# Gates and merge of the mix layers: from feature-major groups of 256 columns to token-major groups of 512

## The chip, the cores and the metric

The kernel runs on one core of one Trainium2 chip. The metric is the device time of one execution in microseconds (us). The core has five engines with queues of their own: PE (matrix products; its weight loads are shown apart as PEld), DVE (vector), ACT (activation functions and copies), POOL and SP (here the issuer of the weight loads). Matrix products are written to PSUM, of which the kernel uses eight banks of 128 partitions x 512 f32 values in the mix layers.

## The reference

The model is a stack of six layers on 256 tokens of width 1024: mix, feed-forward, mix, mixture of experts, and two more. The change touches the two mix layers only. Cut to what matters:

```python
h = _rmsnorm(x, norm_mix[l])
p_rw, p_sb, p_ret, p_conv = jnp.split(h @ w_in[l], MIX_SPLITS, axis=-1)
branches = (rwkv7(p_rw), stick_breaking(p_sb), retention(p_ret), conformer_conv(p_conv))   # each 256 x 256
merged = sigmoid(h @ w_gate[l, 0]) * (branches[0] @ w_branch[l, 0])
for i in range(1, 4):
    merged = merged + sigmoid(h @ w_gate[l, i]) * (branches[i] @ w_branch[l, i])
x = x + merged @ w_out[l]
```

Each gate is a product 256 x 1024 by 1024 x 1024, each branch product 256 x 256 by 256 x 1024. The sigmoid is computed as (1 + tanh(z/2)) / 2, and the last factor of one half is applied once, when the merged features are split.

## The kernel before

All large products are done in three passes of reduced-width f32 (`mm3`, L302): every operand z is split (`split`, L291) into a high part by ACT and the rest, a low part, by DVE, and high x high, high x low and low x high are added in PSUM. The weights come as raw blocks of 128 x 1024 f32 (512 KB) by DMA from SP's queue (L166) into four buffers, and are split into three pairs of buffers (`whi`, `wlo`); `_WS.next` hands out the next 128, 256 or 512 columns of a block. The normed input is kept feature-major, as tiles `hh` and `hl` of 128 features x 8 chunks x 256 tokens.

There are two forms of product. `gemm_f` is feature-major: a block of 128 x 128 weights is stationary and the 256 tokens stream, so its result has features on partitions; a group has two feature chunks, 2 x 8 x 3 matmuls, in one PSUM bank. `gemm_t` is token-major: 128 tokens of `hh`/`hl` are stationary and 512 weight columns stream; its result has tokens on partitions, and it fills two banks, one for each half of the tokens, step by step in turn. Both take their banks from the pool `mmt` of three banks. The other five banks are those of the mixers: three in the lane `mr` (RWKV) and two in the lane `mx`.

In `mix_layer` the generator `jobs` issues the input products and then the gates 3, 2, 1 (L640 is their tanh, into the tiles `gth`). Beside it the four mixers run as threads, which are let in between two steps of a product. L627 and L631 are the evacuations of the three products ahead of the gates (rq twice, and the retention gate `gs`, whose tanh at L631 needs the buffer `w0`, which the convolution's norm uses too). Then `merge` issues, in the order of the list `MERGED`, gate 0 (its tanh is L660) and the branch products in quarters of 256 features: first the four quarters of gate 0, then for each quarter the branches 2, 1, 3 and, one quarter later, 0. DVE multiplies each branch product by its gate (L664) and adds it to the sum (L666); after branch 0 of a quarter, the sum is split (L293, L294) into `m`, which is feature-major and so is right away the stationary operand of the output projection `out_proj` (matmuls `op`): it streams 512 columns of `w_out` for two halves q of the columns, eight chunks k and two halves t of the tokens.

The order in an engine's queue is not the program's order alone: when the kernel is built, instructions of each engine are put in order by priority (early in the program first) and by when a simulated timeline has their inputs and buffers ready.

Of the kernel before, what the change touches and what calls it, by code (L numbers as in the profile page):

```python
# [11 lines left out]
F32 = mybir.dt.float32  # L12
F32R = mybir.dt.float32r
BF16 = mybir.dt.bfloat16
I32 = mybir.dt.int32
AF = mybir.ActivationFunctionType
ALU = mybir.AluOpType
# [3 lines left out]
T = 256  # L21
D = 1024
KT = 8
# [13 lines left out]
W1 = 7  # L37
MERGE = 2, 1, 3, 0

MERGED = [(None, _c) for _c in range(4)]  # L40
for _c in range(4):
    MERGED += [(_i, _c) for _i in MERGE[:-1]] + [(MERGE[-1], _c - 1)] * (_c > 0)
MERGED += [(MERGE[-1], 3)]
RW_SCALE = 0.606531
NEWTON = -0.703952253
SS_SCALE = 1.0 / (16.0 * -NEWTON ** 3)
# [163 lines left out]
class _K:  # L210
# [166 lines left out]
        return ps  # L377


    def gemm_t(self, ws, h, part=lambda t: slice(t * 128, (t + 1) * 128)):  # L380
        hh, hl = h
        if ws.w == 512:
            ps = [self.mmt("gt").rearrange("p a b -> p (a b)") for t in range(2)]
            for k in range(KT):
                w = ws.next()
                for t in range(2):
                    self.mm3(ps[t], hh[:, k, part(t)], hl[:, k, part(t)], *w, k == 0, k == KT - 1)
                    yield
            return ps
        ps = self.mmt("gt")  # L390
        blocks = [ws.next() for k in range(KT)]
        for t in range(2):
            s = part(t)
            for k in range(KT):
                self.mm3(ps[:, t, :], hh[:, k, s], hl[:, k, s], *blocks[k], k == 0, k == KT - 1)
                yield
        return ps
# [85 lines left out]
        self.scaled = xi  # L483
        return last

    def out_proj(self, ap, h, nk=KT, norm=True, out=None, skew=2, spare=()):

        nc = self.nc
        hh, hl = h
        skew += len(spare)  # L490
        ws = _WS(self, ap, 512, {nk - skew + i: z for i, z in enumerate(spare)})
        ps = {}

        def products(t, q, k, w):
            s = slice(t * 128, t * 128 + 128)
            if (t, q) not in ps:
                ps[t, q] = self.mmt("op").rearrange("p a b -> p (a b)")
            return self.mm3(ps[t, q], hh[k][:, s], hl[k][:, s], *w, k == 0, k == nk - 1)

        def finish(t, q):  # L500
            c = slice(q * 512, q * 512 + 512)
            self.held["add"] = nc.vector.tensor_add(self.x[:, t, c], self.x[:, t, c], ps[t, q])
            if out is not None:
                nc.sync.dma_start(out.rearrange("(t p) d -> p t d", t=2)[:, t, c], self.x[:, t, c])
            elif norm:
                self.summed = (self.sumsq(t, q, ps[t, q]),)

        late = []
        for q in range(2):
            for k in range(nk):  # L510
                w = ws.next()
                products(0, q, k, w)
                yield
                if q * nk + k >= 2 * (nk - skew):
                    late.append((q, k, w))
                else:
                    products(1, q, k, w)
                    yield
            finish(0, q)
            if q == 0 and not late:  # L520
                finish(1, q)
        for q, k, w in late:
            self.held["mm", (q - 2) * nk + k + 2] = products(1, q, k, w)
            yield
            if k == nk - 1:
                finish(1, q)
        if not late:
            finish(1, 1)


    def mix_layer(self, l):
        nc, tc = self.nc, self.tc
        with ExitStack() as ctx:
            p = lambda name, **k: _Pool(ctx.enter_context(tc.tile_pool(name=self.nm(name), reuse_waits="tile", **k)))

            bp, gp, lp = p("bp", bufs=1), p("gp", bufs=3), p("lp", bufs=1)
# [33 lines left out]
            wi, wg = self.a[f"w_in_{l}"], self.a[f"w_gate_{l}"]  # L570
            xn = gp.tile([128, 2, D], F32, tag="gth", name=self.nm("xn"))
            h = self.norm_tiles()
            brt = lambda tag: lp.tile([128, 2, 2, T], F32R, tag=tag, name=self.nm("br"))
            br, gth = [None] * 4, [None] * 4

            def jobs():
# [12 lines left out]
                for i in range(4):  # L589
                    ps = yield from self.gemm_f(wf, h)  # L590
                    for j in range(2):
                        f = 2 * i + j
# [39 lines left out]
                nc.vector.scalar_tensor_tensor(gs, th, 1.0, ps, op0=ALU.add, op1=ALU.mult)  # L632
                ret.append((rq, gs))
                for i in (3, 2, 1):
                    gth[i] = gp.tile([128, 2, D], F32, tag="gth", name=self.nm("gth")).rearrange(
                        "p a (b c) -> p (a b) c", c=T)
                    ws = _WS(self, wg[8 * i - 8:8 * i], 128)
                    for fp in range(4):
                        ps = yield from self.gemm_f(ws, h)
                        nc.scalar.activation(gth[i][:, 2 * fp:2 * fp + 2, :], ps, AF.Tanh, scale=0.5)  # L640

            ret = []

# [4 lines left out]

            def merge():

                ws = _WS(self, self.a[f"w_merge_{l}"], 128)
                q4 = self.tp.tile([128, 2, 2, T], F32, tag="q4", name=self.nm("g0"))
                g0 = [self.tp.tile([128, 2, T], F32, tag=n, name=self.nm("g0")) for n in ("hs", "hc")] + [q4[:, 0], q4[:, 1]]
                mg, mh, ml = gth[MERGE[0]], [], []
                for i, fp in MERGED:
                    s = slice(2 * fp, 2 * fp + 2)
                    o = mg[:, s, :]
                    if i is None:
                        ps = yield from self.gemm_f(ws, h)
                        nc.scalar.activation(g0[fp], ps, AF.Tanh, scale=0.5)  # L660
                        continue
                    gt = gth[i][:, s, :] if i else g0[fp]
                    ps = yield from self.gemm_f(ws, (br[i][:, 0], br[i][:, 1]), 2)
                    nc.vector.scalar_tensor_tensor(gt, gt, 1.0, ps, op0=ALU.add, op1=ALU.mult)  # L664
                    if i != MERGE[0]:
                        nc.vector.tensor_add(o, o, gt)  # L666
                    if i == MERGE[-1]:
                        m = self.rp.tile([128, 2, 2, T], F32R, tag=("MB", "Tn", "Tt", "AR")[fp], name=self.nm("m"))
                        self.split(o, m[:, 0], m[:, 1], scale=0.5)
                        for j in range(2):  # L670
                            mh.append(m[:, 0, j, :])
                            ml.append(m[:, 1, j, :])
                pair = lambda *t: lambda: [lp.tile([128, D], F32R, tag=n, name=self.nm("wx")) for n in t]
                yield from self.out_proj(self.a[f"w_out_{l}"], (mh, ml), spare=(pair("C", "E"), pair("A", "B")))

            self.run(jobs())
            self.run(merge())
# [1206 lines left out]
def _blocks(w, n, order="f"):  # L1884

    k, c = w.shape
    b = w.reshape(k // 128, 128, c // n, n)
    b = b.transpose(1, 2, 0, 3) if order == "f" else b.transpose(1, 0, 2, 3)
    return np.ascontiguousarray(b.reshape(128, -1, min(1024, b[0].size)).transpose(1, 0, 2))


def _pack(i):
# [6 lines left out]
    for l in range(L):  # L1899
        w = i["w_in"][l]  # L1900
        col = lambda a, b: w[:, a * 256:b * 256]
        f[f"w_in_{l}"] = np.concatenate(
            [_blocks(col(0, 4), 128), _blocks(col(11, 13), 128), _blocks(col(7, 9), 128), _blocks(col(10, 11), 128),
             _blocks(np.concatenate([col(9, 10), col(6, 7)], 1), 512), _blocks(col(4, 6), 512)], 0)
        f[f"w_gate_{l}"] = np.concatenate([_blocks(i["w_gate"][l, b], 128) for b in range(1, 4)], 0)
        wb, g0 = i["w_branch"][l], i["w_gate"][l, 0]
        f[f"w_merge_{l}"] = np.concatenate(
            [_blocks((g0 if b is None else wb[b])[:, 256 * c:256 * c + 256], 128).transpose(1, 0, 2).reshape(128, -1)
             for b, c in MERGED], 1).reshape(128, -1, 1024).transpose(1, 0, 2).copy()
        f[f"w_out_{l}"] = _blocks(i["w_out"][l], 512)  # L1910
        lo = np.zeros((128, 768), np.float32)
        lo[0:64, 0:256] = i["rw_w2"][l]
        lo[64, 0:256] = i["rw_w0"][l]
        lo[64:128, 256:512] = i["rw_a2"][l]
        lo[:, 512:768] = i["rw_g2"][l]
        f[f"lora_{l}"] = lo
        two = lambda v: np.concatenate([v, v])[:, None]
        f[f"par1_{l}"] = np.concatenate(
            [_fm(i["rw_mu"][l]), _fm(i["rw_a0"][l]), _fm(i["rw_k_k"][l]),
             _fm(i["rw_k_a"][l]), _fm(i["rw_r_k"][l].reshape(-1)), _fm(i["rw_ln_w"][l]), _fm(i["rw_ln_b"][l]),  # L1920
             two(i["sb_q_norm"][l]), two(i["sb_k_norm"][l]), _fm(i["ret_gn"][l]), _fm(i["conv_b"][l]),
             _fm(i["conv_ln_w"][l]), _fm(i["conv_ln_b"][l]),
             i["conv_dw"][l].T.reshape(2, 128, 31).transpose(1, 0, 2).reshape(128, 62)], 1)
# [64 lines left out]
```

## Time and profile before

| | us |
|---|---|
| median of 3 runs (1624.14 to 1625.99) | 1625.78 |
| the profiled execution | 1624.98 |
| its span, first to last instruction | 1622.8 |
| PE busy | 1590.9 |
| DVE busy | 1236.9 |
| ACT busy | 949.4 |

An engine's busy time counts instructions in flight. Matmuls are pipelined, so a busy PE is not PE at its peak: the time between the starts of two matmuls says more than the duration of one. In rows of a timeline the columns are the start in us, the duration in us, the engine, the line, the operation, the output and its inputs by the program's names, the shapes, the count, and in brackets the idle time before it with what ended that.

### The profile page before, as it was taken

How to read it: one execution, taken by the hardware profiler on the slowest of the kernel's cores; microseconds unless marked ns; L12 is line 12 of the kernel's file. 1: busy time of each engine (PE TensorE's matmuls, PEld its weight loads, DVE VectorE, ACT ScalarE, POOL GpSimd, SP SyncE). 2: the span in 40 equal slices, each digit the busy share in tenths (PEclk: the TensorE clock that was granted, in tenths of full speed). 3: DMA queues.
4: the chain of work that ended last, by engine and by line, in shares of the span. 5: the costliest groups of instructions: out<-in, count | busy, mean ns of one | idle time of the engine just before them, and what ended most of it. 6: DMA issues, size and time to landing. Idle time of an engine off the chain costs nothing.

```text
span 1622.8 us, 28866 instructions
## 1 busy us (share of the span) xinstructions
PE 1590.9 (98%) x11229; PEld 1394.3 (86%) x11229; DVE 1236.9 (76%) x2017; ACT 949.4 (59%) x1414; POOL 98.2 (6%) x183
## 2 busy tenths in 40 slices
PE   7999999999999999998999999999999999999998
PEld 6999998999889999997788788888789987888887
DVE  5698678655565996687989989899877776796775
ACT  4545444544446464345877878878756565554654
POOL 2000000100000000001000000100110000010020
PEclk9999999999999999999999999999999999999999
DMA  7443345555555433354989989999754343444342
GB/s 272 154 179 108 118 140 185 200 183 182 195 169 183 169 126 110 120 177 171 349 314 337 362 307 345 353 330 362 266 169 156 116 145 119 141 167 137 129 143 91
DMA packets 89452, 323.71 MB, mean 199 GB/s; under 512 B 10208, under 2 KB 10384, under 8 KB 89312
## 3 DMA queue, kind: packets, MB, share of 16 engines
q1 hardware_dynamic: 86832, 313.89, 55.3%
q0 software_dynamic: 1616, 5.47, 1.0%
q10 hardware_dynamic: 864, 2.47, 0.4%
q8 instruction: 89, 1.46, 0.4%
q14 instruction: 51, 0.42, 0.1%
HBM read 320.74 MB, written 1.05 MB: 198 GB/s over the span
## 4 chain that ended last, share of the span: by engine, by line
PE 49%; DVE 2%; issue 1%; ACT 1%; DVEq 0%; ACTq 0%
PE eg L302 13%; PE gt L302 10%; PE ye L302 7%; PE gf L302 7%; PE op L302 3%; PE s L302 2%; DVE wlo L291 1%; PE seg L302 1%; PE sc L302 1%; PE ms L302 1%; PE xg L302 1%; PE mo L302 1%; PE ut L313 1%; PE qkT L313 1%; ACT whi L291 0%
## 5 line engine op out<-in xcount | busy, mean ns | idle before, releaser
L291 DVE TENSOR_TENSOR wlo<-raw,whi 128x1024 fp32r<-128x1024 f32 x579 | 704.7, 1228 | 256.1 <-ACT whi L291 246.0
L291 ACT ACTIVATE whi<-raw 128x1024 fp32r<-128x1024 f32 x579 | 608.2, 1059 | 413.2 <-PE gf L302 148.2
L302 PE MATMUL gf<-hh,whi 128*128 128x256 f32 x1408 | 400.9, 285 | 0.1
L302 PE MATMUL gf<-hh,wlo 128*128 128x256 f32 x1408 | 400.9, 286 | 0.0
L302 PE MATMUL gf<-hl,whi 128*128 128x256 f32 x1408 | 400.7, 285 | 0.0
L302 PEld LDWEIGHTS gf<-hl,whi 128*128 128x128 f32 x1408 | 269.5, 191 | 2.9 <-issue 1.5
L302 PEld LDWEIGHTS gf<-hh,wlo 128*128 128x128 f32 x1408 | 268.6, 191 | 3.6 <-issue 1.8
L302 PEld LDWEIGHTS gf<-hh,whi 128*128 128x128 f32 x1408 | 269.5, 191 | 1.9 <-issue 0.4
L302 PE MATMUL eg<-wlo,Xh 128*128 128x512 f32 (+1 forms) x384 | 145.8, 380 | 3.2 <-DVE wlo L291 3.2
L302 PE MATMUL eg<-whi,Xl 128*128 128x512 f32 (+1 forms) x384 | 144.1, 376 | 0.0
L302 PE MATMUL eg<-whi,Xh 128*128 128x512 f32 (+1 forms) x384 | 140.1, 382 | 1.4 <-DVEq L1289 1.4
L302 PE MATMUL gt<-whi,hh 128*128 128x512 f32 (+1 forms) x368 | 128.3, 354 | 2.6 <-ACT whi L291 1.5
L302 PE MATMUL gt<-wlo,hh 128*128 128x512 f32 (+1 forms) x368 | 129.7, 353 | 1.1 <-DVE wlo L291 1.1
L302 PE MATMUL gt<-whi,hl 128*128 128x512 f32 (+1 forms) x368 | 128.5, 350 | 1.4 <-DVE hl L291 1.4
L302 PEld LDWEIGHTS eg<-wlo,Xh 128*128 128x128 f32 x384 | 72.1, 188 | 19.8 <-DVE wlo L291 7.3
L302 PEld LDWEIGHTS eg<-whi,Xh 128*128 128x128 f32 x384 | 72.1, 188 | 15.3 <-ACTq L1289 1.6
L302 PEld LDWEIGHTS eg<-whi,Xl 128*128 128x128 f32 x384 | 72.4, 189 | 12.6
L302 PEld LDWEIGHTS gt<-whi,hh 128*128 128x128 f32 x368 | 70.3, 192 | 12.9 <-ACT hh L291 2.2
L302 PEld LDWEIGHTS gt<-whi,hl 128*128 128x128 f32 x368 | 70.3, 191 | 12.4 <-DVE hl L291 2.7
L302 PEld LDWEIGHTS gt<-wlo,hh 128*128 128x128 f32 x368 | 70.5, 192 | 11.2 <-DVE wlo L291 1.9
L302 PE MATMUL ye<-wlo,uh 128*128 128x512 f32 x176 | 69.2, 393 | 0.0
L302 PE MATMUL ye<-whi,ul 128*128 128x512 f32 x176 | 69.0, 392 | 0.0
(516 smaller groups left out, 2431.9 us busy)
## 6 DMA issues: line engine op xcount, KB each, us to landing
raw<-in_moe_w SPq DMA_DIRECT2D x264, 512.0 KB, 5.2
raw<-in_ffn_w SPq DMA_DIRECT2D x66, 512.0 KB, 3.3
raw<-in_even_w_in SPq DMA_DIRECT2D x65, 512.0 KB, 3.3
raw<-in_w_in SPq DMA_DIRECT2D x52, 512.0 KB, 4.2
raw<-in_w_gate SPq DMA_DIRECT2D x48, 512.0 KB, 3.2
raw<-in_w_merge SPq DMA_DIRECT2D x32, 512.0 KB, 3.2
raw<-in_odd_w_in SPq DMA_DIRECT2D x32, 512.0 KB, 3.3
raw<-in_w_out SPq DMA_DIRECT2D x16, 512.0 KB, 3.2
```

Source lines behind the costliest of these rows:

```text
L291: return nc.scalar.activation(hi, src, AF.Copy), nc.vector.tensor_sub(lo, src, hi.bitcast(F32))
L302: return self.nc.tensor.matmul(out, lhsT, rhs, **kw)
L313: return self.nc.tensor.transpose(out, z, self.c("ident") if ident is None else ident)
```

## The change

The gates 3, 2, 1, gate 0 and the branch products become token-major with 512 columns: `gemm_t` with the normed input (or a branch) stationary, in halves c of 512 features. `gemm_t` gets a number of chunks `nk` and a `lane`: for the branch products (nk=2) the bank of the second token half comes from the lane `mx`. `MERGED` gets a new order: half 0 of gate 0, branches 2, 1, 3 of half 0, half 1 of gate 0, branch 0 of half 0, then branches 2, 1, 3, 0 of half 1. The merged sum now has tokens on partitions, so `turn(c)` transposes it on PE, 128 x 128 at a time, into a bank of the lane `mr`, and splits it from there: `turn(0)` stands ahead of the third last group of the list, `turn(1)` in the output projection ahead of chunk 4. The host packs the same weights in the new order.

```diff
-MERGED = [(None, _c) for _c in range(4)]
-for _c in range(4):
-    MERGED += [(_i, _c) for _i in MERGE[:-1]] + [(MERGE[-1], _c - 1)] * (_c > 0)
-MERGED += [(MERGE[-1], 3)]
+MERGED = [(None, 0)] + [(_i, 0) for _i in MERGE[:-1]] + [(None, 1), (MERGE[-1], 0)] + [(_i, 1) for _i in MERGE]
+TURN = 3
...
-    def gemm_t(self, ws, h, part=lambda t: slice(t * 128, (t + 1) * 128)):
+    def gemm_t(self, ws, h, part=lambda t: slice(t * 128, (t + 1) * 128), nk=KT, lane=None):
         hh, hl = h
         if ws.w == 512:
-            ps = [self.mmt("gt").rearrange("p a b -> p (a b)") for t in range(2)]
-            for k in range(KT):
+            ps = [self.mx("gt", lane) if t and lane else self.mmt("gt").rearrange("p a b -> p (a b)") for t in range(2)]
+            for k in range(nk):
                 w = ws.next()
                 for t in range(2):
-                    self.mm3(ps[t], hh[:, k, part(t)], hl[:, k, part(t)], *w, k == 0, k == KT - 1)
+                    self.mm3(ps[t], hh[:, k, part(t)], hl[:, k, part(t)], *w, k == 0, k == nk - 1)
...
-    def out_proj(self, ap, h, nk=KT, norm=True, out=None, skew=2, spare=()):
+    def out_proj(self, ap, h, nk=KT, norm=True, out=None, skew=2, spare=(), before=None):
...
             for k in range(nk):
+                if before and q == 0 and k == before[0]:
+                    before[1]()
                 w = ws.next()
...
-                    gth[i] = gp.tile([128, 2, D], F32, tag="gth", name=self.nm("gth")).rearrange(
-                        "p a (b c) -> p (a b) c", c=T)
-                    ws = _WS(self, wg[8 * i - 8:8 * i], 128)
-                    for fp in range(4):
-                        ps = yield from self.gemm_f(ws, h)
-                        nc.scalar.activation(gth[i][:, 2 * fp:2 * fp + 2, :], ps, AF.Tanh, scale=0.5)
+                    gth[i] = gp.tile([128, 2, D], F32, tag="gth", name=self.nm("gth"))
+                    ws = _WS(self, wg[8 * i - 8:8 * i], 512)
+                    for c in range(2):
+                        ps = yield from self.gemm_t(ws, h)
+                        for t in range(2):
+                            nc.scalar.activation(gth[i][:, t, 512 * c:512 * c + 512], ps[t], AF.Tanh, scale=0.5)
...
-                ws = _WS(self, self.a[f"w_merge_{l}"], 128)
+                ws = _WS(self, self.a[f"w_merge_{l}"], 512)
...
+                M = [[self.rp.tile([128, 4, T], F32R, tag=n, name=self.nm("m")) for n in z] for z in (("MB", "Tn"), ("Tt", "AR"))]
+
+                def turn(c):
+                    for t in range(2):
+                        ps = self.mx("mT", "mr").rearrange("p (k t) -> p k t", k=4)
+                        for k in range(4):
+                            self.tr(ps[:, k], mg[:, t, 512 * c + 128 * k:512 * c + 128 * k + 128])
+                        s = slice(128 * t, 128 * t + 128)
+                        self.split(ps, M[c][0][:, :, s], M[c][1][:, :, s], scale=0.5)
+
+                for n, (i, c) in enumerate(MERGED):
+                    if n == len(MERGED) - TURN:
+                        turn(0)
                     if i is None:
-                        ps = yield from self.gemm_f(ws, h)
-                        nc.scalar.activation(g0[fp], ps, AF.Tanh, scale=0.5)
+                        ps = yield from self.gemm_t(ws, h)
+                        for t in range(2):
+                            nc.scalar.activation(g0[2 * c + t], ps[t], AF.Tanh, scale=0.5)
                         continue
-                    gt = gth[i][:, s, :] if i else g0[fp]
-                    ps = yield from self.gemm_f(ws, (br[i][:, 0], br[i][:, 1]), 2)
-                    nc.vector.scalar_tensor_tensor(gt, gt, 1.0, ps, op0=ALU.add, op1=ALU.mult)
-                    if i != MERGE[0]:
-                        nc.vector.tensor_add(o, o, gt)
-                    if i == MERGE[-1]:
-                        m = self.rp.tile([128, 2, 2, T], F32R, tag=("MB", "Tn", "Tt", "AR")[fp], name=self.nm("m"))
-                        self.split(o, m[:, 0], m[:, 1], scale=0.5)
-                        for j in range(2):
-                            mh.append(m[:, 0, j, :])
-                            ml.append(m[:, 1, j, :])
+                    ps = yield from self.gemm_t(ws, (br[i][:, 0], br[i][:, 1]), nk=2, lane="mx")
+                    for t in range(2):
+                        o = mg[:, t, 512 * c:512 * c + 512]
+                        gt = gth[i][:, t, 512 * c:512 * c + 512] if i else g0[2 * c + t]
+                        nc.vector.scalar_tensor_tensor(gt, gt, 1.0, ps[t], op0=ALU.add, op1=ALU.mult)
+                        if i != MERGE[0]:
+                            nc.vector.tensor_add(o, o, gt)
+                for m in M:
+                    mh += [m[0][:, k] for k in range(4)]
+                    ml += [m[1][:, k] for k in range(4)]
...
-                yield from self.out_proj(self.a[f"w_out_{l}"], (mh, ml), spare=(pair("C", "E"), pair("A", "B")))
+                yield from self.out_proj(self.a[f"w_out_{l}"], (mh, ml), spare=(pair("C", "E"), pair("A", "B")),
+                                         before=(4, lambda: turn(1)))
```

## Rows read from the trace of the kernel before

**Rows 1.** The page: busy time of each engine over the span.
```profile
PE 1590.9 (98%) x11229; PEld 1394.3 (86%) x11229; DVE 1236.9 (76%) x2017; ACT 949.4 (59%) x1414; POOL 98.2 (6%) x183
```
**Rows 2.** Busy us by stage, first mix layer: PE, PEld, DVE, ACT, POOL, clock, DMA.
```profile
97.30:172.00 74.70, 74.70 (x1123) 70.05 (x1122) 64.80 (x129) 42.86 (x65) 2.68 (x4) 1.00 0.38 134
...
235.60:259.20 23.60, 23.41 (x194) 23.09 (x193) 22.23 (x31) 10.45 (x12) 0.00 (x0) 1.00 0.53 178
259.20:282.00 22.80, 21.46 (x89) 16.50 (x90) 18.83 (x28) 11.34 (x16) 0.00 (x0) 1.00 0.63 202
```
**Rows 3.** Timeline of PE, gates: first and last of 31 matmuls in a row.
```profile
169.73 0.28 PE L302 MATMUL gf<-hl,whi 128*128 128x256 f32 x1
...
173.32 0.28 PE L302 MATMUL gf<-hl,whi 128*128 128x256 f32 x1
```
**Rows 4.** Timeline of PE, sbqk product: first and last of 31 matmuls in a row.
```profile
71.69 0.39 PE L302 MATMUL gt<-whi,hl 128*128 128x512 f32 x1
...
78.51 0.39 PE L302 MATMUL gt<-whi,hl 128*128 128x512 f32 x1
```
**Rows 5.** Timeline of PE, output projection: first and last of 12 matmuls in a row.
```profile
260.21 0.39 PE L302 MATMUL op<-wlo,m 128*128 128x512 f32 x1
...
262.78 0.40 PE L302 MATMUL op<-wlo,m 128*128 128x512 f32 x1
```
**Rows 6.** Timeline of PE, expert layer: six transposes and the products after them.
```profile
822.91 0.38 PE L313 MATMUL ut<-cst,u 128*128 128x128 f32 x2
823.13 0.60 PE L313 MATMUL pt<-cst,pw 128*128 128x128 f32 x4
823.49 0.48 PE L302 MATMUL eg<-whi,Xh 128*128 128x512 f32 x1
823.80 0.39 PE L302 MATMUL eg<-wlo,Xh 128*128 128x512 f32 x1
```
**Rows 7.** Timeline of ACT, evacuations before the gates; then L631 by source, both layers.
```profile
91.53 0.58 ACT L627 ACTIVATE rq<-gf 128x512 f32<-128x512 f32 x1
103.05 0.58 ACT L640 ACTIVATE gth<-gf 128x512 f32<-128x512 f32 x1
...
L631 ACT ACTIVATE th<-gf x2: 598/599/600, 171.8 to 631.8; 128x512 f32<-128x512 f32 x2
```
**Rows 8.** Timeline, end of gate 0's last group: PE goes on, ACT's next two.
```profile
235.62 0.40 PE L302 MATMUL gf<-br,whi 128*128 128x256 f32 x2
235.75 1.06 ACT L291 ACTIVATE whi<-raw 128x1024 fp32r<-128x1024 f32 x1 [1.82 <-PE gf L302]
...
236.71 0.58 ACT L660 ACTIVATE g<-gf 128x512 f32<-128x512 f32 x1
```
**Rows 9.** Timeline of DVE: the last writes of branch 2 and of branch 0.
```profile
214.50 0.69 DVE L291 TENSOR_TENSOR br<-y,br 128x512 fp32r<-128x512 f32 x1
...
230.10 0.42 DVE L291 TENSOR_TENSOR br<-d,br 128x256 fp32r<-128x256 f32 x1 [0.48 <-ACT br L291]
```
**Rows 10.** Timeline of DVE in the merge, three instructions in a row.
```profile
255.44 1.22 DVE L291 TENSOR_TENSOR wlo<-raw,whi 128x1024 fp32r<-128x1024 f32 x1
256.57 0.68 DVE L664 SCALAR_TENSOR_TENSOR gth<-gth,gf 128x512 f32<-128x512 f32 x1
257.17 0.69 DVE L666 TENSOR_TENSOR gth<-gth,g 128x512 f32<-128x512 f32 x1
```
**Rows 11.** Timeline of PE, output projection: the two products that waited for DVE.
```profile
259.20 0.47 PE L302 MATMUL op<-whi,m 128*128 128x512 f32 x1 [0.20 <-DVE gth L664]
...
268.39 1.43 PE L302 MATMUL op<-wx,m 128*128 128x512 f32 x5 [0.79 <-DVE wx L291]
```
**Rows 12.** Timeline, norm of the next layer: transposes on PE, high part, low part.
```profile
282.58 0.66 PE L313 MATMUL xt<-cst,xn 128*128 128x128 f32 x4
283.27 0.60 ACT L291 ACTIVATE hh<-xt 128x512 fp32r<-128x512 f32 x1 [2.98 <-PE xt L313]
...
283.90 0.69 DVE L291 TENSOR_TENSOR hl<-xt,hh 128x512 fp32r<-128x512 f32 x1 [0.71 <-ACT hh L291]
```

More of the change, by code (lines that the diff above doesn't have):

```diff
@@ L649, in merge @@
             def merge():
-                ws = _WS(self, self.a[f"w_merge_{l}"], 128)
-                q4 = self.tp.tile([128, 2, 2, T], F32, tag="q4", name=self.nm("g0"))
-                g0 = [self.tp.tile([128, 2, T], F32, tag=n, name=self.nm("g0")) for n in ("hs", "hc")] + [q4[:, 0], q4[:, 1]]
+                ws = _WS(self, self.a[f"w_merge_{l}"], 512)
+                q4 = self.tp.tile([128, 2, 512], F32, tag="q4", name=self.nm("g0"))
+                g0 = [self.tp.tile([128, 512], F32, tag=n, name=self.nm("g0")) for n in ("hs", "hc")] + [q4[:, 0], q4[:, 1]]
@@ L654, in merge @@
                 mg, mh, ml = gth[MERGE[0]], [], []
-                for i, fp in MERGED:
-                    s = slice(2 * fp, 2 * fp + 2)
-                    o = mg[:, s, :]
+                M = [[self.rp.tile([128, 4, T], F32R, tag=n, name=self.nm("m")) for n in z] for z in (("MB", "Tn"), ("Tt", "AR"))]
[6 more added lines that the diff above has]
+                        self.split(ps, M[c][0][:, :, s], M[c][1][:, :, s], scale=0.5)
@@ L1904, in _pack @@
              _blocks(np.concatenate([col(9, 10), col(6, 7)], 1), 512), _blocks(col(4, 6), 512)], 0)
-        f[f"w_gate_{l}"] = np.concatenate([_blocks(i["w_gate"][l, b], 128) for b in range(1, 4)], 0)
+        f[f"w_gate_{l}"] = np.concatenate([_blocks(i["w_gate"][l, b], 512) for b in range(1, 4)], 0)
         wb, g0 = i["w_branch"][l], i["w_gate"][l, 0]
         f[f"w_merge_{l}"] = np.concatenate(
-            [_blocks((g0 if b is None else wb[b])[:, 256 * c:256 * c + 256], 128).transpose(1, 0, 2).reshape(128, -1)
-             for b, c in MERGED], 1).reshape(128, -1, 1024).transpose(1, 0, 2).copy()
+            [_blocks((g0 if b is None else wb[b])[:, 512 * c:512 * c + 512], 512) for b, c in MERGED], 0)
         f[f"w_out_{l}"] = _blocks(i["w_out"][l], 512)
```

## The prediction

> **What bounds the kernel now.** I read the page first: PE has work in flight for 98% of the span [rows 1], so the question is what PE's own queue costs. Then the stage table of the first mix layer [rows 2]; the second repeats it 460 us later (the two evacuations of L631 are such a pair [rows 7]). While the gates run beside the four mixers, PE is busy for all of the 74.7 us. In the merge (235.6 to 259.2) it is busy 23.41 of 23.60 us, with DVE at 22.23: two engines are nearly full. In the output projection, 259.2 to 282, PE is idle 1.34 us, and the waits name DVE [rows 11]. The granted clock is 1.00 in all these rows (2.4 GHz), so no stage has a clock to gain or lose. So this change is worth what it takes off PE's queue, less the waits it makes.
>
> **What is taken off PE.** Per mix layer the three early gates are 3 x 8 feature chunks x 8 k x 3 products = 576 matmuls of 256 columns, gate 0 is 192, and the branch products are 4 x 8 x 2 x 3 = 192: 960, and 1920 in both layers. After, 128 tokens are stationary and 512 weight columns stream: 960 matmuls of 512 columns in all. The columns streamed are the same; what can differ is the cost of a start. The 256-column stream goes from 169.73 to 173.32 us in 30 steps, 0.1197 us each [rows 3], or 0.2394 per 512 columns. For 512 columns there are two prices. The existing 512-column product of the same normed input in this stage takes 6.82 us for 30 steps, 0.2273 each [rows 4]; the output projection, on other stationary tiles, takes 2.57 us for 11 steps, 0.2336 [rows 5]. The gates have the operands of the first (hh and hl stationary, split weights streaming [rows 4]), so I take 0.2273: 768 x 0.0121 = 9.3 us. The 192 branch products have mixer outputs as stationary operand, which no row shows: between 192 x 0.0121 = 2.3 and 192 x 0.0058 = 1.1, I take 1.7. Sum **-11.0 us**; with every product at 0.2336 it is 960 x 0.0058 = 5.6, with all at 0.2273 it is 11.6.
>
> Between one 512-column matmul and two of 256 lie 12 ns [rows 3, 4]. The Trainium skill, "TensorE: Matmul & The Clock Gate", section "Back-to-back issue gap", gives 262 warm cycles for 256 columns and 518 for 512. That leaves 2.5 ns per pair, 2.4 us over 960 pairs instead of 11.0, and the change would lose to its transposes. The trace disagrees with both figures (0.1197 and 0.2273 us, 287 and 546 cycles), so the rows decide.
>
> Loads from memory are as many and as large as before (24, 16 and 8 of 512 KB per layer in gates, merge and projection), in a new order of the host's packing; SP's queue gains and loses nothing. ACT's tanh count stays (24 for gates 1 to 3 and 8 for gate 0, 512 elements each), and so do DVE's multiply-adds, adds and splits. They cost nothing new because their number and shapes stay; what moves is when they free a bank.
>
> **What is added to PE.** Four turns, two per layer, of 8 transposes of 128x128 f32. Six such transposes inside a 512-column stream took 823.49 - 822.91 = 0.58 us, and the first product after them 0.31 instead of 0.23 [rows 6]: 0.66 for six, 0.11 each, 32 x 0.11 = **+3.5 us**. The section "PE-mode transpose" of the same page of the Trainium skill has about 275 ns for one in a kernel. By that the turns would take 8.8 us; the trace shows less than half of it, 0.11 each [rows 6].
>
> **What is added in waits.** (a) PSUM banks of the gates. A 256-column group filled one of three banks; now a group fills two at once. And one bank is not free: the third product of the rq loop has its evacuation (L631) only at 171.8 us, though it was computed between the evacuations of 91.53 and 103.05 (two groups of 48 x 0.12 = 5.76 us lie between) [rows 7]. So from about 97 to 172 us only two banks rotate, in the second layer likewise (631.8). That did no harm before, since a group needed one. After, of the six new gate groups about four changes from group to group fall in that stretch per layer, eight in all. At a group's end T, token half 0 has been complete for 0.7 us (three products); its tanh (0.58) ends near T. Half 1 comes at T. In the row of a group's end PE goes on at 235.62, ACT starts the next weight split at 235.75 and the tanh only at 236.71 [rows 8]. If that order stays, half 1's bank is free at T + 0.13 + 0.97 + 0.58 = T + 1.7, and PE wants it at T + 0.7: 1.0 us each, 8 in all. If the tanh goes first it is free at T + 0.7: nothing. If both halves' tanh fall behind the split, PE can't start at all before T + 1.67: 1.6 each, 13 in all. The queues are ordered at build time by what is ready, so PE may take half 0's next k step first, and small mixer products fill gaps. I take 0.3 each, **+2.4**, between 0 and 13. Behind the waiting product queue the mixers' small products.
>
> (b) Start of the merge. Branches 2, 1, 3 now come after one half of gate 0, 48 x 0.23 = 11 us, not after 23 us. Branch 2 is written at 214.50 and branch 0 at 230.10, and gate 0 began near 208: its four groups end at 235.62, 4 x 5.76 of their own and about 5 of mixer products before that [rows 8, 9]. Branch 2 is first needed near 222 and branch 0 past 235. Both are in time. But a branch group costs DVE 1.13 (weight split) + 4 x 0.60 (by the starts in [rows 10]) = 3.5 us against 12 x 0.23 = 2.8 on PE, and the RWKV tail is on DVE then. The second half of gate 0 behind it (11 us of PE for 4.5 of DVE) absorbs it unless its low weight parts come late: 0 to 1.5 per layer, I take 0.25, **+0.5**.
>
> (c) The second turn. Before it DVE owes 18 multiply-adds and adds (10.8), the first turn's two low parts (1.2) and about five weight splits (5.7): 17.7 us, against 20.5 on PE: five groups of 2.8, the first turn's 0.9 and the projection's 24 products ahead of chunk 4, 5.6. DVE's work for the last group comes only at the end, so it is just in time. Then the chain: transposes, ACT's high part, DVE's low part; in the norm of the feed-forward layer 282.58, 283.27, 283.90 [rows 12]. PE covers part of it with the second token half's transposes (0.43): high part 0.13 + 0.60 - 0.43 = 0.30, and the low part (0.69 behind it, against two products of 0.23) 0.2 more, 0.5. With a weight split and two adds ahead on DVE it is 2.3 more. I take 1.0 per layer, **+2.0**, between 1.0 and 5.6.
>
> **What goes.** With half of gate 0 in the middle, DVE recovers between branch groups, and the projection starts on a half turned long before. The waits of 0.20 for a last group and 0.79 for a weight part behind DVE's backlog [rows 11] should go: **-2.0** for two layers, between 0 and 2.5.
>
> **Sum.** -11.0 + 3.5 + 2.4 + 0.5 + 2.0 - 2.0 = -4.6 us. On the profiled execution, 1624.98 (span 1622.8 and 2.2 around it), that is 1620.4. The median of the three runs is 0.8 above that execution, so **1621.2**.
>
> **The rivals.** All are worked on 1621.2.
> - *Two banks are too few* (the other side). ACT runs the split of the next weights ahead of both tanh, so every one of eight group changes costs 1.6 us: 13 instead of 2.4, 1631.8. For it: the order at the end of gate 0's last group [rows 8]. Against: half 0 is complete 0.7 us before that split can start. It decides from 2.4 / 8 + 4.6 / 8 = 0.9 us per change. Chance 0.08. Half 1 alone behind the split, 1.0 each: 1626.8, within the noise of no change, 0.10.
> - *The wide stream goes at the slower pace.* All 960 products take 0.2336 [rows 5]: 5.6 instead of 11.0, 1626.6. For it: that stretch follows the merge directly, with DVE still behind. Against: the same operands at 0.2273 [rows 4]. Chance 0.12. By the figures of the Trainium skill's page named above the two streams would differ less still.
> - *DVE becomes the bound of the merge.* The second turn comes 3 us late per layer and the second gate half 1.5: +4 and +2.5, 1627.7. For it: 22.23 of 23.60 [rows 2]. Against: DVE's total doesn't grow and PE's breathing space lies better. Chance 0.08.
> - *Everything is hidden.* No bank wait (-2.4), no start wait (-0.5), branch products at 0.2273 (-0.6), the turn at 0.5 (-1.0), and the 192 projection matmuls, whose stationary tiles are laid out anew, at 0.2273 (192 x 0.0063 = -1.2): 1615.5. Chance 0.12.
> - The forecast holds the remaining 0.50; its own range is 1618 to 1623.5.
>
> **Numbers.** About 0.2%, 3.25 us, is what a measurement of this kernel can tell from no change. Faster: the forecast less a tenth of it, the hidden case and a little of the slow pace, 0.58. Slower: the first rival and the edges of the half-bank and DVE cases, 0.12. Same: the rest, 0.30. The range from 1615 to 1629 takes in all but the first rival and the tails of the others.
>
> **What would show it.** gt rows of 512 columns in the gates 0.227 us apart (pace); a wait on ACT's gate tanh before the second token half of a group, between about 97 and 172 us (banks); the first turned group with no PE wait before the next branch group; a wait of 0.5 to 1 us after the second turn's transposes (turn); the projection's later products without the wait on DVE's wx. PE idle beyond 1 us at each group change, or a 512-column pace near 0.234, would make the prediction wrong.

## The result, and the profile after

The change makes the kernel slower: 1648.15 us median of four runs (1647.81 to 1649.37) against 1625.53 of four runs of the kernel before in the same job; ratio 1.0142, 95% interval 1.0127 to 1.0158. The prediction of 1621.2 us (1615 to 1629) was wrong in sign.

The page of the kernel after (first its busy line, as [rows 1]; then one of the costliest groups, with busy time, mean ns and idle time before it):

```profile
PE 1594.4 (97%) x10301; PEld 1350.2 (82%) x10301; DVE 1236.4 (75%) x2017; ACT 954.4 (58%) x1418; POOL 99.4 (6%) x183
...
L300 PE MATMUL gt<-whi,hh 128*128 128x512 f32 (+1 forms) x624 | 228.0, 375 | 7.7 <-ACT gth L641 4.6
```

928 matmuls fewer on PE (960 products saved, 32 transposes added), and yet PE is in flight 3.5 us longer (1594.4 against 1590.9), and its share of the longer span falls from 98 to 97%. The stage table says where (stretches of the first mix layer, columns as [rows 2]):

```profile
210.00:217.50 7.50, 7.50 (x59) 6.06 (x58) 6.26 (x20) 3.37 (x5) 0.00 (x0) 1.00 0.24 82
217.50:222.60 5.10, 0.98 (x7) 0.58 (x5) 4.84 (x17) 1.28 (x3) 0.00 (x0) 1.00 0.29 103
222.60:225.40 2.80, 2.78 (x7) 2.21 (x8) 1.02 (x2) 0.00 (x0) 0.00 (x0) 0.51 0.00 0
...
262.40:288.00 25.60, 25.14 (x112) 19.61 (x110) 19.65 (x24) 12.00 (x16) 0.00 (x0) 1.00 0.66 217
288.00:300.00 12.00, 8.24 (x29) 6.75 (x29) 8.11 (x17) 5.61 (x10) 0.00 (x0) 0.72 0.10 30
```

There are two holes. Where the merge should start, PE works 0.98 of 5.10 us, and the granted clock is 0.51 behind it: the 1.2 GHz level instead of 2.4. Behind the output projection the clock is 0.72 on average. What PE waits for stands in its timeline:

```profile
217.47 0.38 PE L300 MATMUL g<-AR,bt 64*128 64x128 f32 x2
220.36 0.63 PE L311 MATMUL rT<-cst,hc 128*128 128x128 f32 x4 [2.50 <-DVE hc L708]
222.62 0.79 PE L300 MATMUL gt<-whi,br 128*128 128x512 f32 x1 [1.63 <-ACT br L289]
223.21 0.63 PE L300 MATMUL gt<-wlo,br 128*128 128x512 f32 x1
223.63 0.63 PE L300 MATMUL gt<-whi,br 128*128 128x512 f32 x1
...
287.72 0.40 PE L300 MATMUL op<-whi,m 128*128 128x512 f32 x1
291.88 1.12 PE L311 MATMUL xt<-cst,xn 128*128 128x128 f32 x4 [3.76 <-DVE xn L470]
```

At 217.5 PE has run out of gate products and waits for the mixers: for the normed head of retention (`hc`), then for branch 2. At 287.7 it waits for the norm of the next layer, with nothing beside it. In DVE's timeline the last writes of branches 2 and 0, as [rows 9]:

```profile
222.60 0.69 DVE L289 TENSOR_TENSOR br<-y,br 128x512 fp32r<-128x512 f32 x1
...
255.37 0.41 DVE L289 TENSOR_TENSOR br<-d,br 128x256 fp32r<-128x256 f32 x1
```

So branch 2 is 8 us later than before and branch 0 25 us later. Yet the gates are faster. One run of 46 gate products on PE, first and last, as [rows 4]:

```profile
95.69 0.40 PE L300 MATMUL gt<-wlo,hh 128*128 128x512 f32 x1
...
105.92 0.39 PE L300 MATMUL gt<-whi,hl 128*128 128x512 f32 x1
```

10.23 us for 45 steps, 0.2273 each, as predicted. How both can be is seen in a mixer step, `tt` of RWKV, beside the tanh of gates 3 to 1 (first and last start in layer 0; view by tile and by source). Kernel after:

```profile
L300 PE MATMUL tt<-Tt,WG x16: 217/218/268, 189.3 to 190.2; 64*64 64x64 f32 x16
...
L641 ACT ACTIVATE gth<-gt x12: 597/597/600, 105.7 to 189.2; 128x512 f32<-128x512 f32 x12
```

Kernel before:

```profile
L302 PE MATMUL tt<-Tt,WG x16: 218/218/267, 178.3 to 179.2; 64*64 64x64 f32 x16
...
L640 ACT ACTIVATE gth<-gf x12: 579/580/599, 103.1 to 208.4; 128x512 f32<-128x512 f32 x12
```

Before, the last of these tanh starts 30 us behind `tt`; after, it starts 0.1 us ahead of it, so all products of the three gates are through. In PE's queue, the gates have overtaken the mixers. Counted along PE's queue in the two traces, at 2400 columns a us, `tt` stands behind 116.9 us of gate and input columns before and behind 128.2 after. The program text puts `tt` ahead of all gates in both kernels, at the same place; so the difference arises in the build, which orders the queue by its forecast of what is ready when.

### The profile page after: what moved, and what is told of

It reads as the page before. It is cut to its first block, busy times and chain, and to the rows that moved or that the text cites. A ratio compares the mean times of both kernels' runs of the same rounds, so it can differ in the third digit from the quotient of the medians.

```text
span 1645.7 us, 27008 instructions
## 1 busy us (share of the span) xinstructions
PE 1594.4 (97%) x10301; PEld 1350.2 (82%) x10301; DVE 1236.4 (75%) x2017; ACT 954.4 (58%) x1418; POOL 99.4 (6%) x183
## 4 chain that ended last, share of the span: by engine, by line
PE 48%; DVE 3%; ACT 1%; issue 1%; DMA 0%; DVEq 0%; ACTq 0%
PE eg L300 13%; PE gt L300 10%; PE ye L300 7%; PE gf L300 7%; PE op L300 3%; PE s L300 2%; DVE wlo L289 1%; PE seg L300 1%; PE sc L300 1%; PE ms L300 1%; PE xg L300 1%; PE mo L300 1%; PE ut L311 1%; PE qkT L311 1%; ACT whi L289 1%
## 5 line engine op out<-in xcount | busy, mean ns | idle before, releaser
L300 PE MATMUL gf<-hl,whi 128*128 128x256 f32 x896 | 255.2, 285 | 0.0
L300 PE MATMUL gf<-hh,wlo 128*128 128x256 f32 x896 | 255.1, 285 | 0.0
L300 PE MATMUL gf<-hh,whi 128*128 128x256 f32 x896 | 254.9, 285 | 0.1
L300 PE MATMUL gt<-whi,hh 128*128 128x512 f32 (+1 forms) x624 | 228.0, 375 | 7.7 <-ACT gth L641 4.6
L300 PE MATMUL gt<-wlo,hh 128*128 128x512 f32 (+1 forms) x624 | 231.9, 372 | 1.1 <-DVE wlo L289 1.1
L300 PE MATMUL gt<-whi,hl 128*128 128x512 f32 (+1 forms) x624 | 230.4, 370 | 1.2 <-DVE hl L289 1.2
L300 PEld LDWEIGHTS gf<-hl,whi 128*128 128x128 f32 x896 | 171.9, 192 | 2.2 <-issue 1.5
L300 PEld LDWEIGHTS gf<-hh,wlo 128*128 128x128 f32 x896 | 171.6, 192 | 1.7 <-issue 1.0
L300 PEld LDWEIGHTS gf<-hh,whi 128*128 128x128 f32 x896 | 171.9, 192 | 1.2 <-issue 0.5
L300 PEld LDWEIGHTS gt<-wlo,hh 128*128 128x128 f32 x624 | 119.0, 191 | 21.2 <-DVE wlo L289 1.9
```

Source lines behind the costliest of these rows:

```text
L300: return self.nc.tensor.matmul(out, lhsT, rhs, **kw)
```

## The experiments

Theories: **M**, the merge's order (half of gate 0 behind branches 2, 1, 3); **Q**, the mixers' place in PE's queue; **B**, the gates' two PSUM banks; **N**, the late products of the output projection, which no longer cover the next norm. Each ratio compares a run with the kernel before in its own job (1624.8 to 1625.1). What a run wins is counted from the kernel after, 1648.15, in whose job the kernel before stood at 1625.53: by the distance from the kernel before in each job these gains are 0.5 to 0.7 us smaller.

**g0_first**: both halves of gate 0 first.

```diff
-MERGED = [(None, 0)] + [(_i, 0) for _i in MERGE[:-1]] + [(None, 1), (MERGE[-1], 0)] + [(_i, 1) for _i in MERGE]
+MERGED = [(None, 0), (None, 1)] + [(_i, _c) for _c in range(2) for _i in MERGE]
```

> The kernel after, with both halves of gate 0 ahead of all branch products (its weights in that order), nothing else changed. Theory M (the loss is the merge's order: half of gate 0 stands behind branches 2, 1 and 3, so TensorE has nothing to do in layer 0 from 217.6 to 222.6 us and is then for 3 us at the lower clock): the wait of 2.8 + 1.9 us and the slow stretch, some 1.4 us, go in both layers, and the rest of the 22.6 us stays or shrinks with it: at most 1636 us. Theory Q (the loss is the mixers' steps standing later in TensorE's queue, behind more gate products): the filler helps with branch 2, but the mixers' tail is as late as it was, branch 0 (ready near 255 us) is then the one waited for, and half or more of the gain is waited away again: 1639 to 1645 us.

1649.11 us (1.0150, 1.0133 to 1.0167): nothing won. M falls as the whole cause. The wait at branch 2 is gone, and PE's timeline shows it again at branch 0:

```profile
251.82 0.66 PE L311 MATMUL yT<-cst,hc 128*128 128x128 f32 x2 [3.69 <-DVE hc L708]
...
254.33 0.80 PE L300 MATMUL gt<-whi,br 128*128 128x512 f32 x1 [0.99 <-ACT br L289]
```

Q expected this wait, but some gain as well; there was none.

**narrow**: the products of gates 1 to 3 in two halves of 256 columns, into the same banks.

```diff
-                    self.mm3(ps[t], hh[:, k, part(t)], hl[:, k, part(t)], *w, k == 0, k == nk - 1)
-                    yield
+                    if not narrow:
+                        self.mm3(ps[t], hh[:, k, part(t)], hl[:, k, part(t)], *w, k == 0, k == nk - 1)
+                        yield
+                        continue
+                    for c in (slice(0, 256), slice(256, 512)):
+                        self.mm3(ps[t][:, c], hh[:, k, part(t)], hl[:, k, part(t)], w[0][:, c], w[1][:, c],
+                                 k + c.start == 0, k == nk - 1, skip_group_check=True)
+                        yield
...
-                        ps = yield from self.gemm_t(ws, h)
+                        ps = yield from self.gemm_t(ws, h, narrow=True)
```

> The kernel after, with each 512-column product of gates 1 to 3 issued as two of 256 columns into the two halves of the same bank: same tiles, same banks, same tanh, same merge order; 288 products of .2273 us become 576 of .1197 us in each layer, 3.5 us more a layer. Theory Q (wide products put more gate columns ahead of each mixer step): the mixers' steps come again about as early as in the kernel before (layer 0: the last w near 175, tt near 179, the last yT near 228 us instead of 184.6, 189.3 and 251), and 7 us of price are outweighed: 1636 to 1643 us. Theory M (the merge's order alone): nothing is won, the 7 us are lost: 1653 to 1656 us. A third, B (the gates' two banks held by late tanh and table loads): the two waits of 1.4 us stay as well: 1653 to 1656 us.

1642.37 us (1.0106, 1.0089 to 1.0123), 5.8 faster than the kernel after although its gate products cost some 7 us more (an estimate from the two paces, 576 x 0.0121). Only the width differs, and `tt` starts at 182.6:

```profile
L300 PE MATMUL tt<-Tt,WG x16: 218/218/267, 182.6 to 183.5; 64*64 64x64 f32 x16
```

So the width alone moves the mixers in the queue, as Q says; M and B expected 1653 to 1656. But Q had also expected the mixers' end to come back, and it did not: the last parts of branches 2 and 0 were written at 223.4 and 254.5, as late as in the kernel after. What is gone is the hole at the start of the merge: the last gate tanh starts at 213.5 instead of 189.2, and PE is busy for all of 217.5 to 228.

**narrow_g0_first**: both edits.

> Both of the above edits. If Q and M are both at work, their gains add up: no wait of more than 1 us of TensorE on a branch, the first layer's merge begins no later than in the kernel before, and of the 22.6 us there remain the price of the narrow gates against 512 columns (7 us, which the kernel before pays as well), the turns (3.5 us) and the second turn's waits: 1624 to 1632 us. Q alone: near the run with narrow gates (1636 to 1643). M alone: near the run with gate 0 first plus 7 us (1641 to 1643).

1647.19 us (1.0135, 1.0118 to 1.0152): a miss for all theories; gate 0 first costs 4.8 us here. Its trace has a wait for a weight split of the output projection that narrow has not, 5.1 us for both layers; in the first:

```profile
265.51 0.50 PE L300 MATMUL op<-wx,m 128*128 128x512 f32 x1 [2.54 <-ACT wx L289]
```

No run takes this wait away, so it is a reading and not a test.

**before_half**: the control in the kernel before, half of gate 0 behind branches 2, 1, 3.

```diff
-MERGED = [(None, _c) for _c in range(4)]
-for _c in range(4):
-    MERGED += [(_i, _c) for _i in MERGE[:-1]] + [(MERGE[-1], _c - 1)] * (_c > 0)
+MERGED = [(None, 0), (None, 1)]
+for _c in range(2):
+    MERGED += [(_i, _c) for _i in MERGE[:-1]]
+MERGED += [(None, 2), (None, 3), (MERGE[-1], 0), (MERGE[-1], 1)]
+for _c in range(2, 4):
+    MERGED += [(_i, _c) for _i in MERGE[:-1]] + [(MERGE[-1], _c - 1)] * (_c > 2)
 MERGED += [(MERGE[-1], 3)]
```

> The kernel before, with only two of gate 0's four quarters ahead of the branch products of quarters 0 and 1, and the other two behind them, as the kernel after has its halves; still features-major and 256 columns. M: branch 2, ready at 214.5 us in layer 0, is now called for at 211: a wait of 3.5 us or more and a stretch at the lower clock, 5 us a layer: 1633 to 1637 us. Q: the mixers are early enough here, so it costs at most the 3.5 us once a layer and no clock: 1626 to 1632 us.

1622.80 us (0.9986, 0.9976 to 0.9996): even a little faster. With the mixers in time (branch 2 ready at 214.6, its first product at 223.3, no wait between), half of gate 0 behind the branches does no harm.

**placed**: the wide gates, but PE's order written out. The helper `mx` notes the first matmul into each mixer tile; a gate product is queued behind each noted one whose place in the queue of the kernel before (`PLACE`, in us of gate and input columns) is passed.

```diff
+PLACE = {
+    ("bk", 0): 80.4, ("qT", 0): 82.1, ("qT", 1): 82.1, ("w", 0): 87.9, ("tn", 0): 92.6, ("z", 0): 92.6, ("z", 1):
...
+    def placed(self, h, cols):
+        with ExitStack() as ctx:
+            if h is self.own:
+                at = self.done / 2400.0 + 0.1
+                for p, i in self.marks:
+                    if at - 4.0 < p <= at:
+                        ctx.enter_context(self.tc.issue_after(i))
+                self.done += cols
+            yield
...
-                    self.mm3(ps[t], hh[:, k, part(t)], hl[:, k, part(t)], *w, k == 0, k == nk - 1)
+                    with self.placed(h, 1536):
+                        self.mm3(ps[t], hh[:, k, part(t)], hl[:, k, part(t)], *w, k == 0, k == nk - 1)
```

> The kernel after, with its wide gate products, and an order written out for TensorE's queue: no gate product is issued ahead of a mixer step that stands before it, counted in gate columns, in the queue of the kernel before (the step tt then stands behind 117.1 us of gate columns at 2400 a us, as in the kernel before with 116.9; in the kernel after it was 128.2). Theory Q (the mixers' place in the queue is what costs): the mixers' steps come as early as in the kernel before or earlier, without the narrow products' 7 us: 1631 to 1638 us. Rival: the steps stood later because their inputs are later on VectorE and ScalarE; TensorE then waits for them at those places, no time is won, and the waits show ahead of w, tn, tt, x and u: 1648 us or more.

1632.08 us (1.0044, 1.0027 to 1.0061): 16.1 of the 22.6 us. The operations are the same as after; only their order differs. `tt` and the last gate tanh:

```profile
L311 PE MATMUL tt<-Tt,WG x16: 218/218/268, 177.3 to 178.2; 64*64 64x64 f32 x16
...
L675 ACT ACTIVATE gth<-gt x12: 578/597/600, 105.2 to 206.9; 128x512 f32<-128x512 f32 x12
```

The rival (inputs late in any case) falls: put earlier, the steps run earlier, without a new wait ahead of them. The last write of branch 0 starts at 238.5 instead of 255.4.

**late_last**:

```diff
-                products(0, q, k, w)
+                last = products(0, q, k, w)
...
         for q, k, w in late:
-            self.held["mm", (q - 2) * nk + k + 2] = products(1, q, k, w)
+            with self.tc.issue_after(last.ins) if before else ExitStack():
+                self.held["mm", (q - 2) * nk + k + 2] = products(1, q, k, w)
```

> The kernel after, with the late products of the output projection of the mix layers (second token half, last 512 columns) held behind the last product of the first token half, as they stood in the kernel before. Theory N (in layer 0 18 of those 24 products went ahead of the first half's last six, so that nothing covers the next norm): the wait of 4.2 us at 287.7 and the stretch at the lower clock behind it go: 1642 to 1644 us. Rival: the first half's last products wait for their weights in any case, and TensorE waits there instead: 1647 to 1649 us.

1640.51 us (1.0098, 1.0082 to 1.0115): 7.6 us, a little more than N expected. The first transposes of the norm now come without a wait, with late products between them (timeline of PE):

```profile
289.75 0.40 PE L300 MATMUL op<-whi,m 128*128 128x512 f32 x1
289.98 0.60 PE L311 MATMUL xt<-cst,xn 128*128 128x128 f32 x4
290.34 0.48 PE L300 MATMUL op<-whi,m 128*128 128x512 f32 x1
```

**bank**:

```diff
-                th = self.tp.tile([128, 2, 256], F32, tag="w0", name=self.nm("th"))
...
-                nc.scalar.activation(th, ps, AF.Tanh, scale=0.5)
-                nc.vector.scalar_tensor_tensor(gs, th, 1.0, ps, op0=ALU.add, op1=ALU.mult)
+                nc.scalar.activation(gs, ps, AF.Tanh, scale=0.5)
+                nc.vector.scalar_tensor_tensor(gs, gs, 1.0, ps, op0=ALU.add, op1=ALU.mult)
```

> The kernel after, with the tanh of gs written into gs itself instead of a shared scratch tile that comes free only near 181 us, so that the PSUM bank of gs comes free some 70 us earlier and the gates have three banks instead of two. Theory B (two banks are too few): the waits of 1.4 and 1.5 us on ScalarE go in both layers: 1642 to 1645 us. Theory Q: with a third bank still more gate columns stand ahead of the mixers (tt behind 133.5 us of them instead of 128.2), the mixers end later still: 1650 to 1658 us.

1644.79 us (1.0123, 1.0107 to 1.0140): 3.4 us won, as B expected, though the two intervals overlap; the waits on the gates' tanh are gone from the trace. Q's second part was wrong: `tt` is indeed later (194.9), but with the gates done sooner the mixers' last transposes `yT` are not (249.9 against 251.0).

**placed_late_bank**: all three.

> All three edits together: the order written out, the late products behind the first half, the bank of gs freed. If Q, N and B are all at work, their parts add up (some 13, 5 and 5 us of the 22.6): 1622 to 1628 us. If only Q and N: 1627 to 1633 us. If the order alone does nothing: 1642 us or more.

1623.47 us (0.9991, 0.9982 to 1.0001): all 22.6 us are accounted for, and what is left is within the noise of the kernel before. One after the other the edits won 16.1 (placed), 5.7 (placed_late, below) and 2.9; alone, late_last and bank won 7.6 and 3.4, so the parts overlap a little.

**placed_late** (without the bank), **turn_early** (`before=(3, ...)` instead of 4), **before_bank** (the bank edit in the kernel before):

> The order written out and the late products behind the first half, without the freed bank (so placed_late_bank without its third edit). If the bank still costs when the order is held (waits of some 0.7 and 1.5 us a layer are left in the run with the order alone): 1626 to 1629 us, 3 to 5 us above placed_late_bank (1623.5). If these waits only move work that is waited for later anyway: 1623 to 1625 us.

> placed_late_bank with the second turn put one pair of k blocks earlier into the output projection (before its k = 3 instead of its k = 4). If the wait of 1.8 us between the second turn's transposes and the next product is the turn's own latency (split by ScalarE and VectorE), six or more products now stand in it in each layer: 1620.5 to 1622.5 us. Rival: the transposes then wait for the last branch's sums, and the wait only moves: 1623 to 1625 us.

> The kernel before with the bank of gs freed early, as in the run named bank. The gates of the kernel before fill one bank at a time, and no wait on a bank showed there: theory B gives no change, 1624 to 1626 us. Theory Q: more gate columns stand ahead of the mixers (tt behind 121.4 us instead of 116.9), so if anything it is slower: 1625 to 1630 us.

placed_late: 1626.40 (1.0007, 0.9998 to 1.0016); the bank is worth 2.9 us with the order held. turn_early: 1623.97 (0.9992, 0.9983 to 1.0001), no gain. In the queue the turn stayed where it was, behind the same six `wx` products, and so did the wait, so the edit did not test how long the turn takes; it is a third place where the text asks and the build decides:

```profile
261.30 1.67 PE L311 MATMUL op<-wx,m 128*128 128x512 f32 x6 [0.31 <-DVE wx L300]
...
265.38 0.50 PE L311 MATMUL op<-whi,m 128*128 128x512 f32 x1 [1.54 <-ACT m L302]
```

before_bank: 1628.83 (1.0025, 1.0015 to 1.0035), slower, as Q expected, and the gates do overtake: `tt` starts at 182.2 instead of 178.3. But PE does not wait for a branch, as Q has it; in the mix layers its listed waits are those of the kernel before to within 0.2 us. Added up from one start on PE to the next, the mixers' products take 49.7 us a layer instead of 47.9, which makes 3.4 of the 3.8 us. Most of that is in `g` and `rz`. In the kernel before, some of these start within 0.01 us of each other:

```profile
183.11 0.48 PE L302 MATMUL g<-AR,kt 64*128 64x256 f32 x1
183.12 0.48 PE L302 MATMUL rz<-rq 64*128 64x256 f32 x1
```

In before_bank `rz` runs alone in places:

```profile
194.32 0.92 PE L302 MATMUL rz<-rq 64*128 64x256 f32 x4
```

That these lost pairs are the cause is not shown.

**before_mixers_late**: the converse of placed, in the kernel before; a mixer matmul is queued behind the gate product that stands at its place in the queue of the kernel after.

```diff
...
+    def placed(self, h, cols, ins):
+        if h is self.own:
+            self.done += cols
+            for p, i in self.marks:
+                if 0.0 <= p - self.done / 2400.0 < cols / 2400.0:
+                    self.tc.add_manual_dep(i, ins.ins.name, mybir.DependencyInfo(
+                        mybir.DependencyClass.NoSync, mybir.DependencyReason.DATA), reason="placed")
...
-                self.mm3(ps[:, f, :], wh, wl, hh[:, k, :], hl[:, k, :], k == 0, k == nk - 1)
+                self.placed(h, 768, self.mm3(ps[:, f, :], wh, wl, hh[:, k, :], hl[:, k, :], k == 0, k == nk - 1))
...
```

> The converse of the order written out: the kernel before, features-major and 256 columns wide, with each mixer step held behind as many gate columns as stand ahead of it in the kernel after (tt behind 127.8 us of them instead of 116.9). Theory Q: the mixers end some 12 us later, the branches are late for the merge, and TensorE waits in both layers: 1634 to 1644 us. Rival: the place in the queue does not matter to a kernel that has all of gate 0 as filler ahead of the branches: 1624 to 1628 us.

1643.82 us (1.0113, 1.0098 to 1.0128): 18.8 us slower with nothing of the change in it but the order. PE waits inside the merge (235.4 to 267.9), for branch 0, and not at its start:

```profile
249.14 0.69 PE L341 MATMUL yT<-cst,hc 128*128 128x128 f32 x2 [4.92 <-DVE hc L725]
251.44 1.01 PE L313 MATMUL gf<-br,whi 128*128 128x256 f32 x3 [1.61 <-ACT br L302]
```

## Why the prediction was wrong

**The step that failed is (b), the start of the merge.** "Branch 2 is first needed near 222 and branch 0 past 235. Both are in time." The times at which they are ready, 214.5 and 230.1, were taken from [rows 9] as if the mixers kept them. But the change alters the width of the products between which the mixers' steps are queued, and the queue is ordered anew at the build. PE had nothing left but the mixers and branch 2 from 217.6 on, and branch 2's last part was ready at 223.3; branch 0 came 25 us late. The step was given 0.5 us; the order cost 16.1 (placed), and half of gate 0 as the only filler is a minor matter (g0_first, before_half). That the queue is not the program's order alone was known, but none of the rivals moved the mixers. The premise "no stage has a clock to gain or lose" failed with it: behind the wait the granted clock was 0.51 for 2.8 us.

**A part left out: the cover of the next norm.** The late products of the projection were not in the sum at all. They cost 7.6 us (late_last): the wait of 3.76 at 287.7 is gone there, and the granted clock is 1.00 where it was 0.72 on average. How the 7.6 divide between the two was not measured.

**The pace** was right: 0.2273 us for the gates, and 12 branch products in a row took 0.2266 a step. So was the price of a transpose: eight of the second turn took 0.84 us from the first start to the next product's (272.85 to 273.69), 0.105 each. The 275 ns that the prediction sets against its 0.11 do not disagree with the trace, though: by tile, a transpose `mT` lasts 270 to 273 ns, and the 0.11 is the time from one start to the next.

**(a) The banks** were right in size (2.4 predicted; 4.6 us of listed waits on `gth` in the kernel after, of which freeing the bank won 3.4 alone, and 2.9 between placed_late and placed_late_bank). The two group changes of the first layer that wait are in the stretch where the third bank is held, as [rows 7] have it for the kernel before. The mechanism was another than the weight split of [rows 8]. ACT's timeline of the kernel after:

```profile
120.87 0.85 ACT L1010 ACTIVATE e<-e 128x768 f32<-128x768 f32 x1
121.73 1.28 ACT L641 ACT_TABLE_LOAD   x1
123.03 0.60 ACT L641 ACTIVATE gth<-gt 128x512 f32<-128x512 f32 x1
123.64 1.28 ACT L1011 ACT_TABLE_LOAD   x1
124.94 0.94 ACT L1011 ACTIVATE e<-e,cst 128x768 f32<-128x768 f32 x1
125.89 1.28 ACT L641 ACT_TABLE_LOAD   x1
127.19 0.60 ACT L641 ACTIVATE gth<-gt 128x512 f32<-128x512 f32 x1
```

A gate's tanh has come between the exp (L1010) and the logarithm (L1011) of stick-breaking, and each of the three changes (exp to tanh, tanh to logarithm, logarithm to tanh) loads a table, 1.28 us. Before, the two stood side by side, with one load behind them:

```profile
122.56 0.85 ACT L998 ACTIVATE e<-e 128x768 f32<-128x768 f32 x1
123.44 0.94 ACT L999 ACTIVATE e<-e,cst 128x768 f32<-128x768 f32 x1
...
125.35 1.28 ACT L640 ACT_TABLE_LOAD   x1
```

In the kernel after, PE's products waited for those two tanh:

```profile
123.68 0.50 PE L300 MATMUL gt<-whi,hh 128*128 128x512 f32 x1 [1.19 <-ACT gth L641]
...
127.84 0.50 PE L300 MATMUL gt<-whi,hh 128*128 128x512 f32 x1 [1.12 <-ACT gth L641]
```

The Trainium skill, "ScalarE: Activation LUTs", section "Table sets: the hidden batching unit", asks to batch activations by set and has exp and ln in one set; the trace agrees, with no load between L998 and L999. The 2.66 us that this page of the Trainium skill gives for a switch (section "What ACT_TABLE_LOAD costs") do not fit: the tanh at 123.03 starts 1.30 us after its load began, and the exp ahead of the load ends only 0.01 us before it.

**(c) The second turn**: 1.0 per layer was taken; with the order held the wait is 1.54 (turn_early's row above). In the kernel after itself five `wx` products stood behind the turn, and no wait is listed there. Of the waits of [rows 11], 0.31 for `wx` is left of 0.79, and the 0.20 is gone.

**With the order held, how good was the sum?** Predicted -4.6; placed_late_bank stands at -1.35 (the interval is -2.9 to +0.2). The traces show which terms fell short. In the two profiled executions, PE's time in both mix layers, from the first product to the last of the output projection, each step from one start to the next counted for the product that began it:

| us | before | placed_late_bank | difference | in the sum |
|---|---|---|---|---|
| gates and input products | 345.5 | 337.2 | -8.3 | -9.3 and +2.4 for (a) |
| branch products | 47.2 | 44.1 | -3.1 | -1.7 and +0.5 for (b) |
| turns, with the wait behind | 0 | 6.5 | +6.5 | +3.5 and +2.0 for (c) |
| mixers' products | 95.9 | 98.9 | +3.1 | nothing |
| output projection | 48.2 | 47.8 | -0.4 | -2.0 |
| norm's transposes | 5.4 | 5.1 | -0.3 | nothing |
| all | 542.1 | 539.6 | -2.5 | -4.6 |

The term that was put at nothing is the mixers' own small products: in the new order they cost 3.1 us more, of which 1.4 are listed waits for `zc`. The cause of the rest stays open.

The clock does not explain the shortfall, though a first view suggests it. The window behind the expert layer, in the kernel before and in placed_late_bank:

```profile
1171.00:1184.00 13.00, 8.92 (x41) 6.06 (x39) 12.65 (x25) 7.86 (x14) 0.00 (x0) 1.00 0.47 155
```

```profile
1171.00:1184.00 13.00, 10.84 (x40) 7.71 (x37) 10.49 (x18) 6.18 (x11) 0.72 (x3) 0.74 0.60 200
```

Both wait there for the same norm, one at 2.4 GHz, the other partly at 1.2. In these two executions the norm's first transposes start at 1173.74 in the kernel before and at 1170.69 in placed_late_bank, its last at 1183.56 and 1182.32: of a lead of 3.05 us 1.24 are left. But over all its executions the kernel before had a mean granted clock of 0.995 in 38 of 52, as placed_late_bank had in 8 of 10; the profiled execution of the kernel before, with 0.997, is like the other 14 (0.997 or 0.998). Among executions at 0.995 the two kernels stand 1.4 to 1.7 us apart, much as their medians do. So, as far as these means show, the fall of the clock belongs to the execution and not to the change; why it comes in one and not in another stays open. The wide products, with the order held and the bank freed, are worth between nothing and 3 us, and before_half is as fast without them.

## What to carry to other kernels

When an engine's queue is ordered by a forecast at the build, a change of tile width is also a change of order: compare the queue position of the latency-bound chain (here one row, `tt`) before pricing anything. Ready times read from a trace hold only for the queue that the trace ran. If a faster stream makes the whole slower, write the old order out first (placed) and look at the price of the stream afterwards.

## What was not expected of the hardware

After 5.10 us in which PE worked 0.98, the clock was 0.51 of full for 2.8 us, and 512-column products came 0.42 us apart (223.21 and 223.63) instead of 0.23: the wait cost some 1.4 us more than its length. And a freed PSUM bank made a kernel slower by 3.8 us without a new wait on PE (before_bank).
